# Taking a weight page's high and low rooms apart in a planned matmul kernel, with new planner constants

## The chip, the cores and the metric

The kernel runs on one core of a Trainium2 chip. The metric is the device time of one execution in microseconds; the time of a kernel is the median of its runs.

## What is computed

The reference is a two-layer encoder trunk over 256 tokens of width 4096, in float32:

```
for l in range(DEPTH):                       # 2 layers
    h = rmsnorm(x, norm_w[l])
    proj = h @ w_in[l]                       # 256x4096 @ 4096x11264
    aq, ak, av, ag, rq, rk, rv, rg = split(proj)
    a_out = silu(ag) * gqa_attention(rope(rmsnorm(aq)), rope(rmsnorm(ak)), av)   # 16 heads of 128
    r_out = silu(rg) * rmsnorm(bidirectional_retention(rope(rq), rope(rk), rv))  # 8 heads, values of 256
    x = x + concat(a_out, r_out) @ w_out[l]  # 256x4096 @ 4096x4096
return rmsnorm(x, final_norm)
```

Nearly all the arithmetic is in the two projections.

## The kernel before, in words

**Products.** A float32 number is split into a high part (a cast to fp32r) and a low part (the number less its high part), and a product of two numbers is three matmuls on TensorE: high by high, low by high (both at L1458, with the page's high part moving), and high by low (L1468). Each moves 512 columns. The work on one stretch of 1024 output columns is a *block*: 11 blocks for the input projection and 4 for the output projection of each layer, one after the other. A block goes through 16 *pairs* of 128-row strips of the weights. Five or six of the pairs use seven products (Strassen's scheme, with sums of weights), the others eight products with a shared third operand. The products of a block add up in seven PSUM banks, M1 to M7. At the end of the block VectorE and ScalarE drain the banks into two SBUF tiles `ca` and `cb` (`combine`, L1475), and the next block's first product in a bank waits for its drain.

**Pages.** The weights come as pages of 128x1024 numbers. SyncE loads a raw page (`wraw`, five buffers, L447). ScalarE casts it to `whi`, VectorE makes `wlo = wraw - whi`; a seven-product pair has sums in `wsum` between. There are `RING = 5` buffers each of `whi` and `wlo`. Some pages are *far* (`fhi`, `flo`, one buffer, L492): ScalarE makes both the high part and its negative, and a DMA on GpSimd's queue adds the raw weights onto it (L505). `parts` (L473) takes a room for both parts of a page, emits the cast, and puts the making of the low part on a list (`later`) that is worked off when the plan has time, at the latest when TensorE takes the page. `begin` (L510) starts a page; it is called in `end_product` (L1413) when the last product of an older page is finished, that is, after its last L1468 matmul, for the page that comes five later.

**Groups.** The loop at L1438 takes up to `TOGETHER = 4` products that read the same page: first the two L1458 matmuls of each, then the L1468 matmul of each.

**The order.** Every engine's queue is written out in Python, in program order, by a planner. It keeps a model clock (`Now`) that advances 0.2268 us for a matmul of 512 columns, and model clocks of VectorE and ScalarE (`Clock`, with `V_FIXED`, `S_FIXED` and a cost for each element). All other work (splitting the operands for the next phase, rotary embeddings, the attention's scores and values, retention, norms) is written as generators, *lanes*, that yield the time for which they want to rest. After each product `tick` (L892) steps the lanes that are due, as long as `room` (L558) finds that VectorE and ScalarE can take another step (`STEP_V`, `STEP_S`) and still make the coming pages in time, with a reserve of `1.25 + 2 * PASS + MARGIN`, less `RUSH` in the first output block of a layer. In the first `TIGHT_A` and last `TIGHT_B` products of a block a step is taken only if both engines are nearly idle. `need` (L747) and `take` (L544) force work that has come too late. A lane that has a matmul next rests `PE_REST` after its last vector work (L848); a PSUM bank for lanes is taken as free `2 * PASS` after its last reader (L823). A tile stored to HBM and fetched again is expected `FETCH` after the fetch is issued (L1149, L1105), other loads after `LANDING`; a far page `FAR_LANDING` after its cast; the far page's DMA is put into GpSimd's queue when its cast is at most `ADD_AHEAD` away (L555). The constants move no instruction by themselves: a wait in the program is always for the true producer, and the constants decide only in which order the instructions stand.

**Output tasks.** After an output block, `out_tasks` (L1558) issues two DMAs that add the residual, rests `LANDING`, and then runs `out_task` for each of the two 512-column halves.

**Last block.** In the last block, halves of the pages of five pairs are kept until the end in rooms of operands that are no longer needed; `dead_room` (L581) hands these out in an order written as a list of tags.

Of the kernel before, what the change touches and what calls it, by code (L numbers as in the profile page):

```python
# [12 lines left out]
F32R = mybir.dt.float32r  # L13
# [4 lines left out]
P = 128  # L18
# [9 lines left out]
NB = 512  # L28
# [4 lines left out]
NP = KT // 2  # L33
BLK = 32
ALL = slice(None)
# [3 lines left out]
RING = 5  # L39
FAR = 1  # L40

STEP_V = 1.6
STEP_S = 1.3

V_FIXED = 0.15
S_FIXED = 0.12

MM = {512: 0.2268, 256: 0.1177}
PASS = 0.2

LANDING = 11.0
STORE = 8.0
FETCH = 13.0
FAR_LANDING = 11.0
MARGIN = 0.0

RUSH = 1.5

EARLY = 0.7

ADD_AHEAD = 2.5

NEED = {"ak": 4, "ag": 3, "rk": 4, "rg": 4}

PE_REST = 1.5

TIGHT_A = 3
TIGHT_B = 5

AT_ONCE = 2  # L70

WARM = 20

SPLITS = 3

START = 1

# [2 lines left out]
MORE = (1,)  # L80

DELAYED = tuple([_p for _p in range(NP) if _p not in SEVEN + MORE][-5:])
# [129 lines left out]

EASY = ("M7",)

TOGETHER = 4
BANKS = ("M1", "M2", "M3", "M4", "M5", "M6", "M7", "M8")


class Now:


    t = 0.0
# [39 lines left out]
def hybrid_encoder(  # L262
# [15 lines left out]
    now = Now()  # L278
# [16 lines left out]
    def t(pool, shape, tag, bufs=None, dt=F32):  # L295
        kw = {} if bufs is None else {"bufs": bufs}
        return pool.tile(shape, dt, tag=tag, name=tag, **kw)
# [101 lines left out]
    class Weights:  # L399


        def __init__(self):
            self.pages = []
            for l in range(DEPTH):
                for w, n in ((w_in, N_IN), (w_out, N_OUT2)):
                    for b in range(n):
                        second = w is w_out
                        for g in GROUPS[second]:
                            start = (l, b) == (0, 0) and w is w_in
                            for slot in slots_of(g, second, start):  # L410
                                one = Page()
                                one.pair, one.kind, one.uses, one.left = slot[0][1], slot[0][3], len(slot), 3 * len(slot)
                                one.whole = start and one.pair in NATIVE
                                one.seven = one.pair in SEVENS[second] and not one.whole
                                one.far = is_far(g, one.pair, one.kind) and not (
                                    start and (g in GROUPS[0][:2] or one.whole)
                                )
                                one.src, one.begun, one.low_at, one.next = [], False, None, []
                                one.kept = None
                                if w is w_out and (l, b) == (DEPTH - 1, n - 1) and one.pair in DELAYED:  # L420
                                    one.kept = 0 if one.kind == PAGE_A else 1
                                    one.uses, one.left = one.uses - 1, one.left - 3
                                if one.kind == PAGE_A:
                                    one.src.append(w[l, b, one.pair, 0])
                                if one.kind == (PAGE_A if one.seven else PAGE_B):
                                    one.src.append(w[l, b, one.pair, 1])
                                self.pages.append(one)
            self.wholes = [g for g in self.pages if g.whole]
            near = [g for g in self.pages if not g.far and not g.whole]
            far = [g for g in self.pages if g.far]  # L430
            for g, then in zip(near, near[RING:]):
                g.next.append(then)
            for g, then in zip(near[RING : RING + FAR] + far, far):
                g.next.append(then)
            self.order = near[:RING]
            for g in self.pages:
                self.order += g.next
            self.todo = [src for g in self.order for src in g.src]
            self.loaded, self.at = 0, 0
            self.raw, self.later, self.adds = [], [], []  # L440
# [20 lines left out]
                self.later.pop(0)[1]()  # L461
            return self.raw.pop(0)

        def places(self, g, hi, lo, halves=(ALL,)):

            g.hi, g.lo = ({h: v[:, h, :] for h in (0, 1, ALL)} for v in (hi, lo))
            if g.kept is None:
                return halves
            for v in (g.hi, g.lo):
                v[g.kept] = dead_room()  # L470
            return (1 - g.kept, g.kept)

        def parts(self, g, src, halves=(ALL,), then=None):  # L473

            hi = t(wp, [P, 2, NB], "whi", RING, F32R)
            lo = t(wp, [P, 2, NB], "wlo", RING, F32R)
            halves = self.places(g, hi, lo, halves)
            for h in halves:
                ac.copy(g.hi[h], src[:, h, :])
            g.high_at = ac.until + PASS  # L480

            def low():
                ve.after(g.high_at)
                for h in halves:
                    ve.tensor_sub(g.lo[h], src[:, h, :], f32(g.hi[h]))
                g.low_at = ve.until + PASS
                if then:
                    then()

            self.later.append((g, low))  # L490

        def far_parts(self, g, src):  # L492

            hi = t(wp, [P, 2, NB], "fhi", FAR, F32R)
            lo = t(wp, [P, 2, NB], "flo", FAR, F32R)
            halves = self.places(g, hi, lo)
            for h in halves:
                ac.copy(g.hi[h], src[:, h, :])
            for h in halves:
                ac.activation(g.lo[h], f32(g.hi[h]), AF.Copy, scale=-1.0)  # L500
            g.high_at, g.low_at = ac.until, ac.until + FAR_LANDING

            def add():
                for h in halves:
                    nc.gpsimd.dma_start(g.lo[h], g.src[0][:, h, :], accum_op=ALU.add)  # L505

            self.adds.append((ac.until, add))
            self.load()
# [29 lines left out]
                self.later.pop(0)[1]()  # L538

        def low_parts(self, all=False):  # L540
            while self.later and (all or self.later[0][0].high_at <= max(now.t, ve.until) + 0.1):
                self.later.pop(0)[1]()

        def take(self):  # L544
# [34 lines left out]
    rooms = []  # L579

    def dead_room():  # L581

        if not rooms:
            e, o = len(EIGHTS), len(SEVENS[1])
            kinds = {
                "x3": ("x3", e, [P, 2, 2, P], "p k s t -> p (k s t)"),
                "x8h": ("x8h", e, [P, 2, SEQ], "p k s -> p (k s)"),
                "x8l": ("x8l", e, [P, 2, SEQ], "p k s -> p (k s)"),
                "x7h": ("x7h", o, [P, 7, P], "p k t -> p (k t)"),
                "x7l": ("x7l", o, [P, 7, P], "p k t -> p (k t)"),  # L590
            }
            order = "x7h x7l x3 x3 x7h x7l x7h x7l x3 x8h x8l x7h x7l x3 x8h x8l x7h x7l x3 x7h" if MORE else "x3 x3 x8h x8l x3 x3 x8h x8l x7l x7h x3 x3 x8h x8l x3 x3 x8h x8l x7l x7h"
            rooms.extend(kinds[v] for v in order.split())
        tag, bufs, shape, flat = rooms.pop(0)
        return t(ap, shape, tag, bufs, F32R).rearrange(flat)[:, :NB]

# [750 lines left out]
    def block(after_pair, phase, then, first_order=False, order=LAST_ORDER, last=None, plain=False, hurried=False):  # L1347
# [65 lines left out]
        def end_product(n, name, p, index, k, h):  # L1413
            g = pages[p, k]
            follow()
            if n == final[name]:
                finished.append((name, partial(last or combine, name, acc, c)))
                if name == order[0] or n == len(flat) - 1:
                    follow(True)
            if not at_last or name != order[-1] or p not in DELAYED:  # L1420
                g.uses -= 1
            if not g.uses and g in using:
                using.remove(g)
                if g.whole:
                    for _ in range(1 if g is not weights.wholes[-1] else RING):
                        begun()
                for one in g.next:
                    weights.begin(one)
            tick()
            left[p] -= 1  # L1430
            if not left[p]:
                done.append(p)
            while done and all(not left[q] for q in range(min(done))):
                q = min(done)
                done.remove(q)
                after_pair(q)

        n = 0  # L1438
        while n < len(flat):
# [5 lines left out]
            for one in group:  # L1445
# [9 lines left out]
                else:  # L1455
# [3 lines left out]
                    now.t += 2 * MM[NB]  # L1459
                    g.left -= 2  # L1460
                    low.append((one, a[0]))
                    if one is not group[-1]:
                        tick()
            for one, a in low:
# [93 lines left out]
    def out_tasks(l, n, c):  # L1558
        for i in range(2):
            nc.gpsimd.dma_start(c[i], residual(l, 2 * n + i), accum_op=ALU.add)  # L1560
        yield LANDING
        for i in range(2):
            yield from out_task(l, 2 * n + i, c[i])

    def last_combine(res):

# [240 lines left out]
```

## Time and profile before

| | |
|---|---|
| median of 3 runs | 2627.58 us (2625.68 to 2627.82) |
| the profiled execution | 2625.96 us |
| its span, first to last instruction | 2623.8 us |
| TensorE matmul busy | 2601.0 us (99%), 11725 matmuls |
| VectorE busy | 2166.6 us (83%) |
| ScalarE busy | 1804.2 us (69%) |
| GpSimd busy | 372.9 us (14%) |
| mean DMA rate | 261 GB/s, 683.94 MB |

The profile comes from one execution, whose own time is 2.2 us above its span. PE is TensorE's matmuls, DVE VectorE, ACT ScalarE, POOL GpSimd, SP SyncE. L247 is the planner's recording helper, through which all DVE and ACT work goes, so its instructions are told apart by their tiles.

### The profile page before, as it was taken

How to read it: one execution, taken by the hardware profiler on the slowest of the kernel's cores; microseconds unless marked ns; L12 is line 12 of the kernel's file. 1: busy time of each engine (PE TensorE's matmuls, PEld its weight loads, DVE VectorE, ACT ScalarE, POOL GpSimd, SP SyncE). 2: the span in 40 equal slices, each digit the busy share in tenths (PEclk: the TensorE clock that was granted, in tenths of full speed). 3: DMA queues.
4: the chain of work that ended last, by engine and by line, in shares of the span. 5: the costliest groups of instructions: out<-in, count | busy, mean ns of one | idle time of the engine just before them, and what ended most of it. 6: DMA issues, size and time to landing. Idle time of an engine off the chain costs nothing.

```text
span 2623.8 us, 34532 instructions
## 1 busy us (share of the span) xinstructions
PE 2601.0 (99%) x11725; PEld 2154.2 (82%) x11725; DVE 2166.6 (83%) x2684; ACT 1804.2 (69%) x2576; POOL 372.9 (14%) x510
## 2 busy tenths in 40 slices
PE   9999999999999999999999999999999999999998
PEld 7788888888888888888878888888888888888886
DVE  7898887798778898877978878888887688987876
ACT  8676676667565788655877666776576557876655
POOL 0012211221111101111111111211210111010000
PEclk9999999999999999999999999999999999999999
DMA  9988888887778777889988888888877787788887
GB/s 305 285 262 285 272 271 284 270 269 243 235 238 249 239 249 237 274 262 281 311 246 259 271 274 283 266 273 288 280 231 217 245 258 239 221 259 264 254 249 228
DMA packets 201121, 683.94 MB, mean 261 GB/s; under 512 B 24176, under 2 KB 30832, under 8 KB 200944
## 3 DMA queue, kind: packets, MB, share of 16 engines
q1 hardware_dynamic: 147760, 521.27, 56.3%
q0 software_dynamic: 53184, 160.46, 26.5%
q8 instruction: 92, 1.51, 0.2%
q14 instruction: 85, 0.70, 0.1%
HBM read 637.60 MB, written 44.04 MB: 260 GB/s over the span
## 4 chain that ended last, share of the span: by engine, by line
PE 92%; issue 1%; DMA 1%; ACT 1%; DVE 1%; POOL 0%; POOLq 0%; DVEq 0%; ACTq 0%
PE M L1458 59%; PE M L1468 30%; PE ps L973 1%; PE ps L974 1%; PE ps L975 1%; DMA q<-q_dram 1%; PE ps L1458 0%; DMA wraw<-in_w_in 0%; DVE wlo L247 0%; ACT ca L247 0%; DVE ca L247 0%; PE ps L1468 0%; DVE cb L247 0%; ACT pr L247 0%; ACT whi L247 0%
## 5 line engine op out<-in xcount | busy, mean ns | idle before, releaser
L247 ACT CAST whi<-wraw 128x1024 fp32r<-128x1024 f32 (+1 forms) x808 | 768.7, 962 | 463.0 <-PE M L1458 310.3
L247 DVE TENSOR_TENSOR wlo<-wraw,whi 128x1024 fp32r<-128x1024 f32 (+1 forms) x808 | 886.9, 1110 | 236.6 <-ACT whi L247 230.9
L1458 PE MATMUL M<-whi,x8h 128*128 128x512 f32 x1340 | 521.9, 389 | 0.0
L1458 PE MATMUL M<-whi,x8l 128*128 128x512 f32 x1340 | 521.5, 389 | 0.0
L1458 PE MATMUL M<-whi,x7h 128*128 128x512 f32 x1265 | 493.9, 390 | 3.7 <-DVE ca L247 2.5
L1458 PE MATMUL M<-whi,x7l 128*128 128x512 f32 x1265 | 492.9, 390 | 0.0
L247 ACT CAST whi<-wsum 128x1024 fp32r<-128x1024 f32 x314 | 329.6, 1050 | 137.1 <-PE M L1458 93.8
L1468 PE MATMUL M<-wlo,x8h 128*128 128x512 f32 x1340 | 420.2, 389 | 0.0
L247 DVE TENSOR_TENSOR wlo<-wsum,whi 128x1024 fp32r<-128x1024 f32 x314 | 382.5, 1218 | 38.7 <-ACT whi L247 36.8
L1468 PE MATMUL M<-wlo,x7h 128*128 128x512 f32 x1265 | 407.8, 389 | 1.1 <-DVE wlo L247 1.1
L1458 PEld LDWEIGHTS M<-whi,x8h 128*128 128x128 f32 x1340 | 251.6, 188 | 51.7 <-issue 0.2
L1458 PEld LDWEIGHTS M<-whi,x8l 128*128 128x128 f32 x1340 | 251.6, 188 | 51.7 <-issue 0.2
L1468 PEld LDWEIGHTS M<-wlo,x8h 128*128 128x128 f32 x1340 | 251.2, 188 | 51.7
L1458 PEld LDWEIGHTS M<-whi,x7h 128*128 128x128 f32 x1265 | 237.8, 188 | 55.7 <-DVE ca L247 2.9
L1468 PEld LDWEIGHTS M<-wlo,x7h 128*128 128x128 f32 x1265 | 237.5, 188 | 50.5 <-DVE wlo L247 1.5
L1458 PEld LDWEIGHTS M<-whi,x7l 128*128 128x128 f32 x1265 | 238.0, 188 | 48.9
L1458 PE MATMUL M<-whi,x 128*128 128x512 f32 x840 | 258.9, 389 | 0.7 <-ACT whi L247 0.7
L505 POOL DMA_DIRECT2D flo<-in_w_in x108 | 97.3, 901 | 1044.4 <-ACT flo L247 1001.4
L247 ACT CAST fhi<-wraw 128x1024 fp32r<-128x1024 f32 (+1 forms) x148 | 154.7, 1045 | 99.8 <-PE M L1458 93.9
L247 DVE TENSOR_TENSOR wsum<-wraw 128x1024 f32<-128x1024 f32 x157 | 191.2, 1218 | 18.7 <-DMA wraw<-in_w_out 11.3
L1458 PEld LDWEIGHTS M<-whi,x 128*128 128x128 f32 x840 | 157.1, 188 | 32.9 <-ACT whi L247 1.1
L1458 PE MATMUL M<-fhi,x8h 128*128 128x512 f32 x440 | 171.3, 389 | 0.0
(301 smaller groups left out, 3282.9 us busy)
## 6 DMA issues: line engine op xcount, KB each, us to landing
wraw<-in_w_in SPq DMA_DIRECT2D x700, 512.0 KB, 5.0
wraw<-in_w_out SPq DMA_DIRECT2D x256, 512.0 KB, 5.2
flo<-in_w_in POOLq DMA_DIRECT2D x108, 512.0 KB, 7.9
flo<-in_w_out POOLq DMA_DIRECT2D x38, 512.0 KB, 8.8
full<-next_dram POOLq DMA_DIRECT2D x18, 512.0 KB, 7.7
p_dram<-room POOLq DMA_DIRECT2D x64, 128.0 KB, 4.6
pT<-p_dram POOLq DMA_DIRECT2D x16, 512.0 KB, 8.1
next_dram<-room POOLq DMA_DIRECT2D x40, 128.0 KB, 5.9
```

What stands on the lines that cost most here:

```text
L247: return call(out, *args, **kwargs)
L505: nc.gpsimd.dma_start(g.lo[h], g.src[0][:, h, :], accum_op=ALU.add)
L973: nc.tensor.matmul(out, a[0], b[0], start=start, stop=False)
L974: nc.tensor.matmul(out, a[0], b[1], start=False, stop=False)
L975: nc.tensor.matmul(out, a[1], b[0], start=False, stop=stop)
L1458: nc.tensor.matmul(acc[name], a[i], g.hi[h], start=m == first[name] and not i, stop=False)
L1468: nc.tensor.matmul(acc[name], a, g.lo[h], start=False, stop=m == final[name])
```

## The change

A page's high room and low room are taken apart. `begin` may now be called for the next page as soon as the last high matmul of an older page is emitted (`SOON`), with `low_free` false; the low part's room is taken when the low part is made, which waits until the older page's last low matmul is emitted. Thirteen of the planner's constants get other values. The rooms of the last block's kept halves are handed out in the order in which the pairs end. `out_tasks` has a scheduling point between its two DMAs and between its two halves.

```diff
-STEP_S = 1.3
-V_FIXED = 0.15
-S_FIXED = 0.12
+STEP_S = 1.0
+V_FIXED = 0.12
+S_FIXED = 0.15
-PASS = 0.2
+PASS = 0.3
-FETCH = 13.0
-FAR_LANDING = 11.0
-MARGIN = 0.0
-RUSH = 1.5
+FETCH = 11.0
+FAR_LANDING = 13.0
+MARGIN = 0.6
+RUSH = 1.0
-ADD_AHEAD = 2.5
+ADD_AHEAD = 1.5
-PE_REST = 1.5
-TIGHT_A = 3
-TIGHT_B = 5
+PE_REST = 2.0
+TIGHT_A = 4
+TIGHT_B = 2
-SPLITS = 3
+SPLITS = 2
+APART = 0.0
+SOON = True
...
-        def places(self, g, hi, lo, halves=(ALL,)):
-            g.hi, g.lo = ({h: v[:, h, :] for h in (0, 1, ALL)} for v in (hi, lo))
+        def places(self, g, part, v, halves=(ALL,)):
+            v = {h: v[:, h, :] for h in (0, 1, ALL)}
+            setattr(g, part, v)
             if g.kept is None:
                 return halves
-            for v in (g.hi, g.lo):
-                v[g.kept] = dead_room()
+            v[g.kept] = dead_room()
             return (1 - g.kept, g.kept)
         def parts(self, g, src, halves=(ALL,), then=None):
-            hi = t(wp, [P, 2, NB], "whi", RING, F32R)
-            lo = t(wp, [P, 2, NB], "wlo", RING, F32R)
-            halves = self.places(g, hi, lo, halves)
+            halves = self.places(g, "hi", t(wp, [P, 2, NB], "whi", RING, F32R), halves)
             for h in halves:
                 ac.copy(g.hi[h], src[:, h, :])
             g.high_at = ac.until + PASS
             def low():
+                assert g.low_free
+                self.places(g, "lo", t(wp, [P, 2, NB], "wlo", RING, F32R))
                 ve.after(g.high_at)
...
         def low_parts(self, all=False):
-            while self.later and (all or self.later[0][0].high_at <= max(now.t, ve.until) + 0.1):
+            while self.later and self.later[0][0].low_free and (all or self.later[0][0].high_at <= max(now.t, ve.until) + 0.1):
...
                 for one in g.next:
-                    weights.begin(one)
+                    one.low_free = True
+                    if not one.begun:
+                        weights.begin(one)
...
                     low.append((one, a[0]))
+                    if one is group[-1] and g.uses == len(group) and SOON:
+                        for then in g.next:
+                            if not then.far and not then.begun:
+                                then.low_free = False
+                                weights.begin(then)
...
     def out_tasks(l, n, c):
         for i in range(2):
             nc.gpsimd.dma_start(c[i], residual(l, 2 * n + i), accum_op=ALU.add)
-        yield LANDING
-        for i in range(2):
-            yield from out_task(l, 2 * n + i, c[i])
+            if i < 1:
+                yield APART
+        second = now.t + LANDING
+        yield max(0.0, LANDING - APART)
+        yield from out_task(l, 2 * n, c[0])
+        yield max(0.0, second - now.t)
+        yield from out_task(l, 2 * n + 1, c[1])
```

## Rows read from the trace of the kernel before

**Rows 1.** Busy time by stretches: window, us; PE (x), PEld, DVE, ACT, POOL; PEclk, DMA, GB/s.

```profile
0.00:100.00 100.00, 95.97 (x389) 72.72 (x390) 81.35 (x122) 78.55 (x135) 3.84 (x8) 0.99 0.91 309
...
200.00:300.00 100.00, 100.00 (x459) 83.48 (x458) 84.31 (x102) 70.63 (x106) 20.56 (x29) 1.00 0.87 283
...
1300.00:1400.00 100.00, 96.55 (x422) 78.52 (x421) 80.46 (x109) 79.69 (x129) 9.06 (x11) 1.00 0.82 245
...
2600.00:2624.00 24.00, 12.38 (x55) 9.93 (x53) 13.04 (x26) 6.79 (x14) 1.13 (x2) 0.86 0.47 176
sum 2624.00, PE 2601.00 PEld 2154.21 DVE 2166.59 ACT 1804.18 POOL 372.92; mean PE 96.33 PEld 79.79 DVE 80.24 ACT 66.82 POOL 13.81
```

**Rows 2.** What PE waited for: us in total, times, longest us.

```profile
PE M L1468 <- DVE wlo L247: 2.8, 2, 1.7
PE M L1458 <- DVE ca L247: 2.5, 3, 1.0
PE ps L973 <- ACT pr L247: 2.0, 2, 1.0
PE M L1458 <- DVE cb L247: 1.2, 1, 1.2
...
PE M L1458 <- ACT whi L247: 0.7, 1, 0.7
```

**Rows 3.** Timeline of PE at the first block's end (start, us, what); last, granted clock.

```profile
94.40 0.39 PE L1458 MATMUL M<-whi,x7l 128*128 128x512 f32 x1
95.85 0.50 PE L1468 MATMUL M<-wlo,x7h 128*128 128x512 f32 x1 [1.06 <-DVE wlo L247]
97.58 0.50 PE L1458 MATMUL M<-whi,x7h 128*128 128x512 f32 x1 [1.23 <-DVE cb L247]
...
98.30:101.70 3.40, 3.40 (x10) 2.64 (x9) 3.40 (x5) 2.58 (x6) 0.00 (x0) 0.50 1.04 269
```

**Rows 4.** Timeline of ACT and DVE ahead of these waits.

```profile
88.39 1.05 ACT L247 CAST whi<-wraw 128x1024 fp32r<-128x1024 f32 x1 [4.52 <-DMA wraw<-in_w_in]
...
89.47 1.23 DVE L247 TENSOR_TENSOR wlo<-wraw,whi 128x1024 fp32r<-128x1024 f32 x1 [1.85 <-ACT whi L247]
...
94.58 1.22 DVE L247 TENSOR_TENSOR wlo<-wsum,whi 128x1024 fp32r<-128x1024 f32 x1
```

**Rows 5.** Timeline of DVE and PE at a later block's end.

```profile
1316.38 1.22 DVE L247 TENSOR_TENSOR wlo<-wraw,whi 128x1024 fp32r<-128x1024 f32 x1
1317.51 0.68 DVE L247 TENSOR_TENSOR ca<-ca,M 128x512 f32<-128x512 f32 x1
...
1318.25 0.50 PE L1458 MATMUL M<-whi,x7h 128*128 128x512 f32 x1 [1.00 <-DVE ca L247]
```

**Rows 6.** Timeline of ACT and PE at an attention head's scores.

```profile
345.76 0.56 ACT L247 ACTIVATE pr<-ps,st,rs 128x256 f32<-128x256 f32 x1 [2.33 <-DVE st L247]
...
347.01 0.38 PE L973 MATMUL ps<-kv,aqh 128*128 128x256 f32 x1 [1.00 <-ACT pr L247]
```

**Rows 7.** Timeline of ACT and PE early in the second layer.

```profile
1351.61 1.05 ACT L247 CAST fhi<-wraw 128x1024 fp32r<-128x1024 f32 x1
...
1355.97 0.73 PE L1458 MATMUL M<-whi,x 128*128 128x512 f32 x2 [0.71 <-ACT whi L247]
...
1359.83 0.50 PE L1468 MATMUL M<-wlo,x 128*128 128x512 f32 x1 [1.75 <-DVE wlo L247]
```

**Rows 8.** The fetched queries: ACT, PE, DMA's times to landing, ACT's waits.

```profile
517.87 1.14 ACT L247 CAST aqh<-q 128x512 fp32r<-128x512 f32 x2 [4.25 <-DMA q<-q_dram]
...
518.54 0.39 PE L973 MATMUL ps<-kv,aqh 128*128 128x256 f32 x1 [0.19 <-ACT aqh L247]
...
DMA to landing us min/median/max: 5.7/11.3/14.0
...
ACT aqh L247 <- DMA q<-q_dram: 10.2, 4, 4.3
```

**Rows 9.** Waits for a page's old rooms, and GpSimd's waits for far pages.

```profile
POOL flo L505 <- ACT flo L247: 1462.9, 128, 37.6
ACT whi L247 <- PE M L1458: 404.0, 421, 4.7
...
ACT whi L247 <- PE M L1468: 28.7, 13, 4.2
```

More of the change, by code (lines that the diff above doesn't have):

```diff
@@ L417, in __init__ @@
                                 )
-                                one.src, one.begun, one.low_at, one.next = [], False, None, []
+                                one.src, one.begun, one.low_at, one.next, one.low_free = [], False, None, [], True
                                 one.kept = None
@@ L495, in far_parts @@
             lo = t(wp, [P, 2, NB], "flo", FAR, F32R)
-            halves = self.places(g, hi, lo)
+            self.places(g, "hi", hi)
+            halves = self.places(g, "lo", lo)
             for h in halves:
@@ L591, in dead_room @@
             }
-            order = "x7h x7l x3 x3 x7h x7l x7h x7l x3 x8h x8l x7h x7l x3 x8h x8l x7h x7l x3 x7h" if MORE else "x3 x3 x8h x8l x3 x3 x8h x8l x7l x7h x3 x3 x8h x8l x3 x3 x8h x8l x7l x7h"
-            rooms.extend(kinds[v] for v in order.split())
+            for p in range(NP):
+                if p not in EIGHTS:
+                    rooms.extend(kinds[v] for v in ("x7h", "x7l"))
+                else:
+                    rooms.extend(kinds[v] for v in ("x3", "x8h", "x8l")[: 3 if p in EIGHTS[2:] and p not in DELAYED else 1])
         tag, bufs, shape, flat = rooms.pop(0)
```

## The prediction

> **What bounds the kernel now.** I read the busy time by stretches of 100 us first. TensorE is the bound: of the 27 stretches 20 read as the second row here, 100.00 of 100.00, and its idle time is 2623.8 - 2601.0 = 22.8 us in all [rows 1]. Of that 11.6 us lie after the last matmul (12.38 busy in the last 24) and 4.0 in the first 100 us. The change takes no matmul away, so the 11725 matmuls stay as they are, at 0.227 us from start to start where PE runs on. What can be won is what stands between them.
>
> The second view is the list of what PE waited for. It is short: 2.8 us for low parts, 2.5 and 1.2 us for banks being drained, 2.0 us for the softmax's reading of a lane's bank, 0.7 us for a high part [rows 2]. A row's idle time is counted from the modelled end of the matmul before, 0.389 us after its start, so a wait costs 0.389 - 0.227 = 0.16 us more than it shows. The third view is the timeline around each wait. Four kinds come out:
>
> **A, the end of the first block.** From 94.40 to 95.85 and on to 97.58 the matmuls are 1.45 and 1.73 us apart in place of 0.23: 2.7 us lost [rows 3]. The granted clock then reads 0.50, the lower of the two levels, for 3.4 us, which costs half of that, 1.7 us. Together 4.4 us. DVE is behind there: it waited 1.85 us for a cast that waited 4.52 us for a raw page to land, and so made the wanted low part at 94.58, five us later, behind bank drains and weight sums [rows 4].
>
> **B, other block ends.** Three waits for `ca`, 2.5 us [rows 2], with 3 x 0.16 on top 3.0 us. At 1316 DVE made a low part for 1.22 us first and drained the bank after it, and PE waited 1.00 us [rows 5].
>
> **C, scores.** Two waits of 1.0 us, 2.3 us with the 0.16 each: PE stood before the second head's scores until ACT had read the bank of the first [rows 6].
>
> **D, early in the second layer.** 0.71 us for a high part and 1.75 us for a low part, 2.8 us with the 0.16 each [rows 7]. ACT had far pages, squares and copies in its queue ahead of the page.
>
> A to D come to 4.4 + 3.0 + 2.3 + 2.8 = 12.5 us. With 0.7 us lost on a late query (below) it is 13.2 us, 0.5% of the time, and that is the most that any reordering can bring.
>
> **The change, part by part.** *Beginning the high part earlier.* By its words it frees the high room before the group's low matmuls, up to 4 x 0.227 = 0.9 us earlier. The chip does most of that already: ACT waited 421 times for an L1458 matmul to free `whi`, and 13 times for an L1468 one [rows 9]. The wait was always for the old high part's own reader. What the change moves is the cast's place in ACT's queue, ahead of what `tick` steps during the low matmuls, and the planner's belief of when the page is ready, so that the low part follows directly when its room comes free. Where ACT is ahead of PE this gives nothing. Where a page is late it gives between 0 and 0.9 us for each; I take 0.9 for each of D's two waits, cut by the wait itself to 0.7 + 0.9 = 1.6 us. The upper end is all of D, 2.8.
>
> What is queued behind: an early cast that waits for PE holds ACT's later work. The 421 waits are 404.0 us, 0.96 us each [rows 9]. If a score's exponential stands behind such a cast, the next head's scores are late by about that. C shows two such delays; I price a new order at 0.7 us for new delays of this sort, between 0 and four of 1.0 us. The Trainium skill, "TensorE: Matmul & The Clock Gate", section "Architectural detail", says that ACT and DVE are strict first-in-first-out, which speaks against any early start that has to wait. The trace agrees as far as these waits show it. By that rule alone this part would be a loss of up to 4 us, not a gain.
>
> *Reserve in `room`.* It grows by 2 x 0.1 (`PASS`) + 0.6 (`MARGIN`) = 0.8 us for DVE; for ACT 0.3 less of `STEP_S` leaves 0.5 us. In the hurried block it grows by another 0.5 (`RUSH`). `TIGHT_A` 3 to 4 keeps one more product at a block's start free of side work. Against it stands `TIGHT_B` 5 to 2: three products at the end, some 2 us, in which side work may now be put ahead of the drains. For B I take two thirds, 2.0 us of 3.0 (between 0 and 3.0): the reserve of 0.8 us nearly covers waits of 1.0, and the looser end takes some of it back. For A I take half, 2.2 us of 4.4 (0 to 4.4): its root is a raw page that landed late, and raw pages are neither loaded sooner nor given another buffer, but the drains and the low part behind them can be ordered otherwise.
>
> *Scores.* `PE_REST` + 0.5 and the bank's 2 x 0.1 put the product up to 0.7 us later behind other matmuls. For each of C's two waits that is 0.7 of 1.0: 1.4 us (0 to 2.3). Lanes get slower, but they are used many microseconds later.
>
> *Fetches.* `FETCH` 13 to 11 goes the wrong way for the queries: they land 5.7 to 14.0 us after issue, median 11.3 [rows 8]. Already at 13, ACT stood four times, 10.2 us, and the 4.25 us at 517 cost PE 0.7 us (two waits of some 0.2, with the 0.16 each). With the cast placed 2 us earlier that one hold becomes 6.3 us and costs PE 0.7 + 2 = 2.7; the others stay under 4.25 us, which PE's lead in pages bears. So +2.0 us. Ends: 0, if the queries are fetched into a quieter stretch, and 8, if four casts each cost 2 us.
>
> *Far pages.* `FAR_LANDING` + 2 and `ADD_AHEAD` - 1 I cost at nothing: PE has no wait for `flo` [rows 2]. GpSimd stood 1462.9 us before these DMAs, 128 times [rows 9]; issuing them up to 1 us later in the plan shortens the hold for stores and fetches queued behind. If the cover of the far pages' early start went, PE would wait for `flo` by name.
>
> *The rest.* `SPLITS` 3 to 2 lets two operand splits run side by side in place of three; the scheduling points in `out_tasks` put its second DMA on GpSimd's queue a step later; `V_FIXED` and `S_FIXED` change the model by 0.03 us for an instruction. Each only reorders; they are in the 0.7 us. The kept rooms hold what was held before, and the 11.6 us after the last matmul are a chain that no part of the change touches.
>
> **The sum.** - 2.2 (A) - 2.0 (B) - 1.4 (C) - 1.6 (D) + 2.0 (queries) + 0.7 (new delays) = - 4.5 us. Against the profiled execution's own 2625.96 that is 2621.5. The median of the runs is 1.6 us higher, so 2627.58 - 4.5 = 2623.1.
>
> **The rivals.** *Nearly all stalls go.* If the earlier pages and larger reserve also end A, and queries land in time, 8 to 13 us come back: about 2617. For it: all waits are of 1 to 2 us, the size of the reserve added. Against: A hangs on a landing, and it alone holds a third of the sum. *The stalls only move.* Each constant reorders hundreds of instructions, and the list names some ten waits that the old plan did not foresee [rows 2]; a new plan may have its own. About 2627, within 2 us of before. For it: the early start is largely done by the chip already [rows 9]. *Slower: the fetches bind.* If most of the 8 query fetches are met by a cast that was put in ACT's queue too early, holds pass 4.25 us, the point at which PE began to lose [rows 8], and each costs up to 2 us: with half the gains gone that is about + 8 us, 2635. For it: the median landing of 11.3 is above the new 11. Against: landing varies, and four of the eight did not hold ACT even at 13. That the change does nothing can be left out, since the order of all queues changes.
>
> **How the numbers follow.** Forecast 0.50, nearly all 0.18, only moved 0.20, slower 0.12. A measurement of this kernel can tell about 0.2%, 5.3 us, from no change, so faster means under 2622.3. The forecast of 2623.1 lies near that line: with 2.5 us either way it gives 0.20 to faster and 0.30 to same. Faster 0.20 + 0.18 = 0.38, same 0.30 + 0.20 = 0.50, slower 0.12. The range goes from 2616.0, nearly all of the 12.5 us back, to 2630.0, half the fetches' price with no gain.
>
> **What would show it.** Right: PE's idle time near 18 us; the waits for `ca` and for `pr` under 1 us in sum; the early waits of the second layer shortened; the waits for `whi` still on L1458; the hold of ACT for `q` longer than 10.2 us in sum. If clock 0.50 no longer appears after the first block, A is gone and the first rival gains. Wrong: PE waits for `flo`, for `aqh` or for operands (`x8h`, `x7h`) of more than 2 us each, or a list of new waits as long as the old one.

## The result, and the profile after

The changed kernel takes 2631.22 us (median of 12 runs, 2629.77 to 2639.65), the kernel before 2625.96 us (12 runs beside them). The ratio is 1.0025, with an interval of 1.0018 to 1.0033: slower by about 6 us, where 4.5 us less was forecast. The profiled execution of the changed kernel took 2632.53 us, its span is 2630.8 us, 7.0 us more than before.

Busy time by stretches of the changed kernel, columns as in [rows 1]:

```profile
0.00:100.00 100.00, 98.74 (x407) 75.69 (x408) 84.42 (x126) 81.20 (x135) 3.82 (x8) 1.00 0.91 316
...
900.00:1000.00 100.00, 96.58 (x427) 78.98 (x426) 89.27 (x135) 78.32 (x123) 11.99 (x15) 0.98 0.78 243
...
1300.00:1400.00 100.00, 98.10 (x430) 79.97 (x429) 83.12 (x113) 82.66 (x136) 8.82 (x11) 1.00 0.83 249
...
2200.00:2300.00 100.00, 96.62 (x433) 79.37 (x432) 90.10 (x135) 76.57 (x123) 12.02 (x15) 0.98 0.76 237
...
sum 2631.00, PE 2605.12 PEld 2155.49 DVE 2172.11 ACT 1809.59 POOL 369.90; mean PE 96.49 PEld 79.83 DVE 80.45 ACT 67.02 POOL 13.70
```

The first 100 us and the stretch from 1300 are better than in [rows 1] (98.74 after 95.97, 98.10 after 96.55). Two stretches are new among the bad ones, 900 to 1000 and 2200 to 2300, and each also has a mean clock of 0.98. What PE waited for, beside [rows 2]:

```profile
PE M L1468 <- DVE ca L251: 6.8, 4, 2.6
PE M L1483 <- DMA flo<-in_w_out: 1.6, 3, 1.0
PE M L1468 <- DVE cb L251: 1.5, 4, 0.9
...
PE M L1483 <- DMA x7h<-in_w_out: 1.0, 1, 1.0
PE ps L981 <- DVE D L251: 0.9, 2, 0.5
PE ps L983 <- DVE aql L251: 0.8, 4, 0.2
```

(L1468 and L1483 are what L1458 and L1468 were.) The waits for low parts, for `pr` and for `whi` are gone. The wait for `ca` has grown from 2.5 to 6.8 us, its longest from 1.0 to 2.6. Both long ones are at the *hand-over* from the input blocks to the output blocks of a layer. VectorE and PE at the first:

```profile
975.52 0.68 DVE L251 TENSOR_TENSOR ca<-ca,M 128x512 f32<-128x512 f32 x1
976.12 1.22 DVE L251 TENSOR_TENSOR wlo<-wsum,whi 128x1024 fp32r<-128x1024 f32 x1
977.26 1.22 DVE L251 TENSOR_TENSOR wsum<-wraw 128x1024 f32<-128x1024 f32 x1
978.39 0.68 DVE L251 TENSOR_TENSOR ca<-ca,M 128x512 f32<-128x512 f32 x1
...
976.23 0.40 PE L1483 MATMUL M<-wlo,x7h 128*128 128x512 f32 x1
979.22 0.77 PE L1468 MATMUL M<-whi,x7h 128*128 128x512 f32 x1 [2.60 <-DVE ca L251]
```

and the busy time of the 3.4 us after it, columns as in [rows 1]:

```profile
978.90:982.30 3.40, 3.08 (x7) 2.48 (x8) 3.37 (x5) 2.26 (x4) 0.00 (x0) 0.51 0.00 0
```

VectorE has no idle time. Between the two drains into `ca` stand a low part and a weight sum `wsum`, 1.14 us from start to start each. The sum belongs to a page that comes five pages later, and PE stands for the second drain from 976.23 to 979.22, 3.0 us in place of 0.23. The granted clock then reads 0.51, the lower level, for 3.4 us, as it did after the first block before [rows 3]. In the kernel before, the sum stands behind the last drain, and PE does not wait at the same place:

```profile
980.24 0.68 DVE L247 TENSOR_TENSOR ca<-ca,M 128x512 f32<-128x512 f32 x1
980.84 1.22 DVE L247 TENSOR_TENSOR wsum<-wraw 128x1024 f32<-128x1024 f32 x1
...
981.07 0.47 PE L1458 MATMUL M<-whi,x7h 128*128 128x512 f32 x1
```

There `begin` runs in `end_product` after the drain was emitted; in the changed kernel it runs before the low matmuls of the group, and so before the drain. The page that is begun at the end of every block before an output block is the first page of a seven-product pair, whose `begin` starts with this sum.

Counted from start to start, the two hand-overs lose 2.76 + 2.75 us in these gaps, 1.3 us in four smaller ones and 2 x 1.7 us at half clock, 10.2 us in all; the kernel before had 1.0 there (at 2278), so that is some 9 us more. Gone are A with its half clock (4.4 us), C (2.3) and D (2.8), 9.5 us. The 7.0 us of the span are about what is left over: other block ends (+1.6 us), far and kept pages (+3.3), late queries (+1.0) and scores of the retention (+1.3).

### The profile page after: what moved, and what is told of

The parts are those of the page before. It is cut to its first block, busy times and chain, and to the rows that moved or that the text cites. A ratio compares the mean times of both kernels' runs of the same rounds, so it can differ in the third digit from the quotient of the medians.

```text
span 2630.8 us, 34613 instructions
## 1 busy us (share of the span) xinstructions
PE 2605.1 (99%) x11725; PEld 2155.5 (82%) x11725; DVE 2172.1 (83%) x2684; ACT 1809.6 (69%) x2576; POOL 369.9 (14%) x510
## 4 chain that ended last, share of the span: by engine, by line
PE 82%; DMA 5%; DVE 2%; issue 2%; ACT 1%; POOL 0%; POOLq 0%; DVEq 0%; ACTq 0%
PE M L1468 53%; PE M L1483 26%; DMA q<-q_dram 2%; DMA flo<-in_w_out 2%; PE ps L983 1%; PE ps L981 1%; PE ps L982 1%; DVE wlo L251 1%; DMA q_dram<-cb 0%; DMA full<-next_dram 0%; DVE cb L251 0%; DMA wraw<-in_w_out 0%; DMA x7h<-in_w_out 0%; DVE wsum L251 0%; DVE ca L251 0%
## 5 line engine op out<-in xcount | busy, mean ns | idle before, releaser
L1468 PE MATMUL M<-whi,x8h 128*128 128x512 f32 x1340 | 522.1, 390 | 0.0
L1468 PE MATMUL M<-whi,x8l 128*128 128x512 f32 x1340 | 521.7, 389 | 0.0
L1468 PE MATMUL M<-whi,x7h 128*128 128x512 f32 x1265 | 495.0, 391 | 8.5 <-DVE ca L251 6.8
L1468 PE MATMUL M<-whi,x7l 128*128 128x512 f32 x1265 | 493.5, 390 | 0.0
L1483 PE MATMUL M<-wlo,x8h 128*128 128x512 f32 x1340 | 419.0, 389 | 0.0
L1483 PE MATMUL M<-wlo,x7h 128*128 128x512 f32 x1265 | 408.1, 390 | 0.0
L1468 PEld LDWEIGHTS M<-whi,x8h 128*128 128x128 f32 x1340 | 251.7, 188 | 51.1 <-issue 0.2
L1468 PEld LDWEIGHTS M<-whi,x8l 128*128 128x128 f32 x1340 | 251.7, 188 | 51.1 <-issue 0.2
L1483 PEld LDWEIGHTS M<-wlo,x8h 128*128 128x128 f32 x1340 | 251.0, 188 | 51.8
L1468 PEld LDWEIGHTS M<-whi,x7h 128*128 128x128 f32 x1265 | 238.2, 188 | 61.9 <-issue 6.0
L1483 PEld LDWEIGHTS M<-wlo,x7h 128*128 128x128 f32 x1265 | 238.1, 188 | 49.5 <-DVE wlo L251 0.5
L1468 PEld LDWEIGHTS M<-whi,x7l 128*128 128x128 f32 x1265 | 238.4, 188 | 48.6
L1468 PE MATMUL M<-whi,x 128*128 128x512 f32 x840 | 258.9, 389 | 0.0
L1468 PEld LDWEIGHTS M<-whi,x 128*128 128x128 f32 x840 | 157.7, 188 | 32.9 <-ACT whi L251 0.4
L1468 PE MATMUL M<-fhi,x8l 128*128 128x512 f32 x440 | 171.3, 389 | 0.0
```

Of the source, the lines that this page charges most:

```text
L1468: nc.tensor.matmul(acc[name], a[i], g.hi[h], start=m == first[name] and not i, stop=False)
L1483: nc.tensor.matmul(acc[name], a, g.lo[h], start=False, stop=m == final[name])
```

## The experiments

Three theories went into the first four runs. **M**: the early begin puts the weight sum ahead of the last drain, and that is what the change loses. **C**: the new constants let work pile up on VectorE before the hand-over. **F**: the far pages' late landing. Each ratio is against the kernel before.

**Early begin off, new constants kept.**

```diff
-SOON = True
+SOON = False
```

> The changed kernel with the early begin switched off and all thirteen new constants kept. Theory M (the early begin puts a weight sum of 1.1 us ahead of the block's last drain on VectorE, and the half clock follows): the waits for ca near 976 and 2280 us fall from 2.6 us to about 1.5 or less, the clock stays at 1.00 there, and the time falls by 4 to 8 us, to a ratio of about 1.000 against the kernel before. Theory C (the new constants let side work pile up on VectorE before the hand-over, and the sum's place is secondary): the waits at 976 and 2280 stay above 2 us, the ratio stays at 1.002 or more. Theory F (the far pages' late landing is what costs): the waits for flo tell whether the early begin or the constants made them; 3.2 us are at stake.

Measured: 2653.87 us, ratio 1.0101 (1.0083 to 1.0119): 23 us slower than the changed kernel. That is far above what any of the theories gave. The waits at the hand-overs did fall, to 1.44 and 1.45 us, but half clock came at both all the same. PE's waits, the first hand-over and the stretch after it:

```profile
PE ps L981 <- DVE wsum L251: 7.1, 5, 1.5
PE M L1468 <- DVE ca L251: 7.0, 6, 1.7
PE ps L981 <- ACT pr L251: 3.6, 5, 1.0
PE M L1483 <- DVE wlo L251: 2.9, 3, 1.8
...
PE M L1483 <- DMA flo<-in_w_out: 1.9, 2, 1.3
```

```profile
989.77 0.68 DVE L251 TENSOR_TENSOR ca<-ca,M 128x512 f32<-128x512 f32 x1
990.37 1.23 DVE L251 TENSOR_TENSOR wsum<-wraw 128x1024 f32<-128x1024 f32 x1
...
990.60 0.56 PE L1468 MATMUL M<-whi,x7h 128*128 128x512 f32 x1 [1.44 <-DVE ca L251]
...
990.80:994.20 3.40, 3.40 (x9) 2.67 (x9) 3.40 (x4) 2.49 (x4) 0.00 (x0) 0.51 0.01 5
```

Counted from start to start, the two hand-overs lose 9.3 us, though the sum stands behind the drain and no page is begun early. So VectorE also comes late to the drains for a reason that is not the sum's place, as theory C has it. The rest of the plan is another one: the scores (`ps`, L981) wait for VectorE and ScalarE, ten times. This run therefore cannot price the early begin. It has waits for `flo` without it, which speaks against the early begin as their cause.

**New code, constants as before.** All thirteen lines of constants back:

```diff
-STEP_S = 1.0
+STEP_S = 1.3
...
-SPLITS = 2
+SPLITS = 3
```

> The changed kernel's code with the early begin, with all thirteen constants as before. Theory M: both hand-overs from input to output blocks show a wait for ca of 2 us or more and a stretch at half clock, some 5 us each, whatever the constants are; ratio about 1.002. Theory C: no wait for ca over 1.2 us at the hand-overs, ratio 1.000 or less. Theory F: waits for flo of over 1 us in sum if the early begin makes them, none if FAR_LANDING or ADD_AHEAD do.

Measured: 2661.58 us, ratio 1.0126 (1.0105 to 1.0147). The hand-overs lose 4.3 and 4.7 us with half clock, as M expects and C does not. Of the longest wait for `ca`, 2.6 us, the sum accounts for 1.14; the rest comes here under the old constants, so the new constants alone are not what makes VectorE late. And half of the 35 us above the kernel before is something else:

```profile
PE M L1468 <- ACT x L251: 16.7, 2, 8.4
PE M L1468 <- DVE ca L251: 6.5, 5, 2.6
PE M L1483 <- DVE wlo L251: 3.1, 3, 1.7
...
PE M L1483 <- DMA flo<-in_w_in: 1.8, 3, 0.8
```

Twice PE stands 8.4 us for a third operand `x` of the last pairs in the first output block: the plan makes operands too late. `flo` is waited for here too, with the old `FAR_LANDING` and `ADD_AHEAD`.

**Early begin everywhere but at a block's end.** This pair isolates the sum's place: no queue differs from the changed kernel's but VectorE's, and there only by the order of sum and last drain at eight block ends.

```diff
-                    if one is group[-1] and g.uses == len(group) and SOON:
+                    if one is group[-1] and g.uses == len(group) and SOON and n + len(group) < len(flat):
```

> The changed kernel, but without the early begin after the last group of a block; the only difference in any queue is that at eight block ends the last drain stands ahead of the weight sum on VectorE. Theory M: at 976 and 2280 the wait for ca falls by the sum's 1.14 us, from 2.6 to about 1.5, the clock stays at 1.00, and each hand-over loses 2 us in place of 5: 5 to 7 us less in all, ratio about 1.000. Theory C: the waits fall by the 1.14 us alone and the half clock stays: 2.3 us less, ratio 1.0016. Theory F: the waits for flo stay as they are, 1.6 us, in either case.

Measured: 2626.67 us (12 runs), ratio 0.9998 (0.9987 to 1.0008), 4.6 us less than the changed kernel and the same as the kernel before. At the first hand-over:

```profile
975.84 1.22 DVE L251 TENSOR_TENSOR wlo<-wsum,whi 128x1024 fp32r<-128x1024 f32 x1
976.98 0.69 DVE L251 TENSOR_TENSOR ca<-ca,M 128x512 f32<-128x512 f32 x1
977.58 1.22 DVE L251 TENSOR_TENSOR wsum<-wraw 128x1024 f32<-128x1024 f32 x1
...
977.81 0.47 PE L1468 MATMUL M<-whi,x7h 128*128 128x512 f32 x1 [1.46 <-DVE ca L251]
```

and the stretch after the second hand-over, by busy time:

```profile
2277.80:2281.20 3.40, 3.40 (x9) 2.65 (x9) 3.37 (x4) 2.50 (x4) 0.00 (x0) 0.50 0.00 0
```

The wait falls from 2.60 to 1.46, by the sum's 1.14 us, in both places. After the first the clock stays up, as M has it; after the second it reads 0.50 in this execution, as C has it. The two hand-overs lose 6.8 us in place of 10.2. The 4.6 us of time lie between M's 5 to 7 and C's 2.3 and do not choose between them. What the pair shows is the sum's place itself: no other instruction changes its place, the intervals of the two ratios do not overlap, and with the sum behind the drain the change's loss against the kernel before is gone. It does not make the hand-overs what they were: 6.8 us are still lost there, against 1.0 in the kernel before. The waits for `flo`, which theory F left at 1.6 us, are 0.2 us in this trace.

**Early begin at block ends alone**, the same pair in the other direction, against the run with the early begin off:

```diff
-                    if one is group[-1] and g.uses == len(group) and SOON:
+                    if one is group[-1] and g.uses == len(group) and SOON and n + len(group) >= len(flat):
```

> The early begin after the last group of a block alone; against the run with the early begin off, the only difference is the weight sum ahead of the last drain at eight block ends. Theory M: the two hand-overs wait 1.1 us longer for ca, and the half clock comes with it: 4 to 7 us slower than that run. Theory C: 2.3 us slower, and no half clock, or half clock in both.

Measured: 2657.88 us, ratio 1.0116 (1.0098 to 1.0134), 4.0 us above that run: at M's lower end, though the four runs of each (2652.52 to 2657.11 there, 2656.27 to 2660.53 here) cannot tell that from C's 2.3. `ca` is waited for 9.4 us in place of 7.0, and half clock lasts 6.8 us at both hand-overs where it was 3.4. PE's waits, and the busy time of the first such stretch:

```profile
PE M L1468 <- DVE ca L251: 9.4, 6, 2.6
```

```profile
987.70:994.50 6.80, 5.85 (x14) 4.68 (x15) 6.77 (x9) 5.60 (x9) 0.00 (x0) 0.50 0.40 142
```

So in a second plan the same eight swaps cost some 4 us. Not all of it need be theirs: half clock also doubled from 3.4 to 6.8 us at 1332, where no drain was swapped.

**Which bank is waited for.** A next set took the hand-over further. An output block uses M2 with its fifth product and M4 with its seventh, but the block ahead of it finishes M4 first. The swap:

```diff
+        elif order is LAST_ORDER and then % 2 == 0:
+            order = ("M3", "M5", "M2", "M4")
```

Put on the run without the early begin at block ends:

> The run without the early begin at block ends, and before an output block M2 is finished and drained ahead of M4 instead of after it. Theory M (what PE waits for at a hand-over is M2, the last bank drained and the fifth product of the next output block; M4 is the seventh): the waits for ca at 976 and 2280 fall below 0.5 us, no half clock, 3 to 5 us less than that run: about 2623, ratio 0.9985. Rival B (VectorE is behind on all drains there, so PE waits for another bank as long): within 1 us of that run, ratio 1.000.

Measured: 2624.96 us, ratio 0.9999 (0.9990 to 1.0008). At 979 PE now waits 0.21 us for the drain, and no half clock comes at either hand-over (timeline, then busy time):

```profile
977.52 1.22 DVE L251 TENSOR_TENSOR wlo<-wsum,whi 128x1024 fp32r<-128x1024 f32 x1
978.66 0.68 DVE L251 TENSOR_TENSOR ca<-ca,M 128x512 f32<-128x512 f32 x1
...
979.40 0.50 PE L1470 MATMUL M<-whi,x7h 128*128 128x512 f32 x1 [0.21 <-DVE ca L251]
```

```profile
974.00:982.00 8.00, 7.24 (x28) 4.61 (x27) 8.00 (x11) 3.96 (x5) 0.00 (x0) 1.00 0.50 126
```

The place is right, the size was too high: 1.7 us less than without the swap, which the runs can't tell from nothing. The two hand-overs lose 3.6 us in place of 6.8, but the trace of this run also has 1.4 us for a low part at 1253 that the other had not. It is 6 us under the changed kernel and level with the kernel before.

The swap on the changed kernel alone:

> The changed kernel with nothing but M2 finished and drained ahead of M4 before an output block; the weight sum still stands ahead of the last drain, which is now M4's. Theory M: the sum costs nothing where it stands, since M4 is wanted two products (0.9 us or more) later; the hand-overs lose under 1.5 us each in place of 5, about 7 us less than the changed kernel: 2624, ratio 0.999. Rival B: PE waits for M4 instead, 2 us or more with the half clock, ratio 1.002 or more.

Measured: 2626.32 us, ratio 1.0000 (0.9991 to 1.0009), 4.9 us less than the changed kernel. The sum still stands ahead of the last drain, but this is M4's now:

```profile
979.22 1.21 DVE L251 TENSOR_TENSOR wsum<-wraw 128x1024 f32<-128x1024 f32 x1
980.36 0.68 DVE L251 TENSOR_TENSOR ca<-ca,M 128x512 f32<-128x512 f32 x1
...
981.09 0.50 PE L1470 MATMUL M<-whi,x7h 128*128 128x512 f32 x1 [1.34 <-DVE ca L251]
```

PE waits 1.34 us in place of 2.60, and the clock stays at 1.00. It did not cost nothing, as M said, but about half.

The swap on the kernel before:

> The kernel before with M2 finished and drained ahead of M4 before an output block. Theory M: the 1.0 us at 2278 goes, nothing else moves: 0.5 to 2 us less, ratio 0.9995. Rival B: no change at 2278, ratio 1.000.

Measured: 2627.28 us, ratio 1.0002 (0.9992 to 1.0012). The wait at 2278 is gone from the trace, 1.0 us of 2627, and the time cannot show it.

**Is a plan's time the constants' doing?** The first two runs were 23 and 30 us off the changed kernel, so the next ones moved one constant to its neighbour.

```diff
-V_FIXED = 0.12
+V_FIXED = 0.13
```

> The changed kernel with V_FIXED at 0.13 in place of 0.12: the model charges VectorE 10 ns more for an instruction, which is below anything that the engines could feel. Theory L (a plan's time is largely luck of which stalls its order meets, and the constants chosen are one lucky draw): 5 us or more away from the changed kernel, with stalls in other places, though the hand-overs still show the long wait for ca. Theory P (the constants describe the engines, and nearby values give nearby times): within 3 us, ratio 1.0015 to 1.0035.

Measured: 2666.44 us, ratio 1.0153 (1.0137 to 1.0169), 35 us more, for 10 ns in the model. PE waits for third operands in three places:

```profile
PE M L1468 <- DVE x L251: 12.4, 3, 4.4
PE M L1468 <- ACT x L251: 7.7, 3, 2.7
PE M L1468 <- DVE ca L251: 7.6, 5, 2.6
```

The neighbours of the kernel before, `V_FIXED` at 0.14 and 0.16 in place of 0.15:

> The kernel before with V_FIXED at 0.14 in place of 0.15, 10 ns of the model's charge for an instruction of VectorE. Theory L (the chosen constants are a lucky draw, and a neighbour is an ordinary one): 10 us or more above the kernel before. Theory P (nearby values give nearby times): within 4 us of it.

> The kernel before with V_FIXED at 0.16, the neighbour on the other side. Theory L: 10 us or more above the kernel before, with stalls that the other neighbour doesn't have. Theory P: within 4 us.

Measured: 2627.22 us at 0.14, ratio 1.0002 (0.9990 to 1.0013), and 2657.61 us at 0.16, ratio 1.0111 (1.0074 to 1.0147). One neighbour is as good as the kernel before, though much of its order is another, the other 31 us worse, with waits for `x` again (15.8 us on ScalarE's). The changed kernel's other neighbour, 0.11:

> The changed kernel with V_FIXED at 0.11, on the other side from the run at 0.13 that took 35 us more. Theory L: 5 to 40 us above the changed kernel, in other places than that run. Theory P with a limit between 0.12 and 0.13: within 4 us of the changed kernel.

Measured: 2649.19 us, ratio 1.0067 (1.0043 to 1.0091), 18 us above the changed kernel, with hand-overs of 5.8 and 8.3 us and a wait of 2.3 us for `flo`. Of four neighbours three lie 18 to 35 us higher and one level: theory L holds for most, not for each.

**The queries' rest.** One step of the forecast on its own:

```diff
-FETCH = 11.0
+FETCH = 13.0
```

> The changed kernel with FETCH back at 13 and nothing else. The forecast's step (a cast for a late query placed 2 us later holds ScalarE 2 us less): ScalarE's waits for q fall from 20.0 us to about 10, PE's waits for aql go, 1 to 2 us less if the rest of the plan stood still. Theory L: the rest doesn't stand still, and the time lands 5 us or more above the changed kernel.

Measured: 2632.67 us, ratio 1.0027 (1.0014 to 1.0041), the same as the changed kernel. ScalarE's waits for the queries, 20.0 us in seven with `FETCH` at 11, do not occur, and PE's 0.8 us for `aql` neither. The rows of the changed kernel, the last with the times to landing:

```profile
ACT aqh L251: 20.0, 7
...
PE ps L983: 0.8, 4
...
DMA to landing us min/median/max: 5.9/12.4/14.0
```

The 1 us came back and other waits took its place (1.1 us for a high part at 1371, 0.7 us for `flo` at 1710). The hand-overs have their waits of 2.60 and 2.59 us as in the changed kernel, but in this execution the clock stays up after the second:

```profile
2284.90:2288.30 3.40, 3.39 (x15) 2.81 (x16) 3.37 (x5) 1.96 (x4) 0.00 (x0) 1.00 0.12 18
```

**Constants that move nothing.** With all else as in the changed kernel, putting `TIGHT_B` or `STEP_S` alone back leaves every queue of the program as it is, and `ADD_AHEAD` moves a few DMAs on GpSimd's queue alone.

## Why the prediction was wrong

The bound was read rightly: TensorE is busy 99% before and after, nothing of its work changed, and all that moved were waits of up to 3 us and stretches at half clock.

**A** (2.2 of 4.4 us back): under-sized. The first block's end has no wait and no half clock any more, so all of it came back; PE ran through from 93.8 to 100 without a gap. That belongs to this draw of constants: with the new code and the old constants the waits and the half clock are there again, at 94 and 98.5.

**C** (1.4 of 2.3) and **D** (1.6 of 2.8): right in direction, under-sized; both are gone. Together with A some 9 us were gained where 5.2 were forecast.

**B** (2.0 of 3.0 back): this is the step that failed. In its place came a loss of 9 us at the hand-overs and 1.6 us at other block ends. Two things were wrong in it.

The first is what the early begin puts ahead of what. The forecast costed it as a cast on ScalarE and asked what is queued behind that cast. But `begin` issues more than a cast: for the first page of a seven-product pair it issues a sum on VectorE. VectorE is the engine that drains the banks, and it had no idle time at a block's end [rows 4, 5]. The run with the sum moved behind the last drain (4.6 us less) shows this, since no other instruction changes its place; the run with the sum moved ahead in another plan (4.0 us more) and the one with another bank drained last (4.9 us less) agree. The rule of the Trainium skill that the prediction cited ("TensorE: Matmul & The Clock Gate", "Architectural detail": ACT and DVE run their queues strictly in order) was the right rule, weighed on the wrong one of its two engines: the drain behind the sum came 1.14 us later. On ScalarE the early begin cost nothing that shows: 472 casts waited 447.3 us for PE, 0.95 us each, against 421 of 0.96 [rows 9], while the waits for `pr` went.

The second is the larger reserve in `room`, which was to cover waits of 1.0 us. It covered none. Of the three waits for `ca` before, those of 0.59 us at 186 and 1.00 us at 1318 stand as they were, and the third, at 2278, grew:

```profile
181.64 0.50 PE L1468 MATMUL M<-whi,x7h 128*128 128x512 f32 x1 [0.59 <-DVE ca L251]
...
1320.14 0.50 PE L1468 MATMUL M<-whi,x7h 128*128 128x512 f32 x1 [1.01 <-DVE ca L251]
```

The sum's place makes up 3.4 of the 9 us at the hand-overs. The rest, VectorE's coming late to the drains, is there with the early begin off and the new constants (9.3 us), and a wait of 2.6 us is there with the early begin on and the old constants; what makes it was not settled. That the change ends level with the kernel before once the sum is moved is because what A, C and D gave back pays for that rest.

**TIGHT_B** was taken as what speaks against B. Put back alone, it moves no instruction.

**Queries** (+2.0): right mechanism, over-sized. ScalarE's waits doubled from 10.2 us in four [rows 8] to 20.0 us in seven; from start to start PE lost 1.7 us on them in place of 0.7, so 1.0 us more.

**Far pages** (nothing): wrong by 3 us in the profiled execution, 1.6 us of idle for `flo` and 1.0 for a kept half. Runs with either half of the change undone have waits for `flo` too, and the run without the early begin at block ends, with the same GpSimd queue, has 0.2 us of them and 1.1 us for the kept half. Three plans with the old code have 0.9 to 1.4 us for `flo` as well, one of them the kernel before with nothing but the bank swap. What makes them was not settled.

**New delays** (+0.7, up to 4): the retention's scores cost 1.3 us, a wait for VectorE. The price was read off C as a score's exponential standing behind an early cast, and C does not show that: before it ScalarE stood idle 2.33 us for VectorE's `st` [rows 6].

The rival on the slower side named fetches that bind; the loss came by another way, the one the text listed as a wait for drains and took for a gain. The rival of stalls that only move was nearest: some 9 us gone, some 16 us new. And the range rested on the thought that the terms of one plan carry over to the next. The two kernels and their four neighbours, 10 ns apart in one constant, span 40 us, from 2626 to 2666, so the honest spread of "constants chosen anew", without a sight of the new order, reached some 40 us on the slow side, where the range allowed 2.4 us above the median of before (half of the fetches' 8 us, by which it was set, would have been 4).

What stays open: whether beginning high parts early is worth anything by itself. The change with its end of block mended is level with the kernel before, under other constants; the same constants without it are 27 us slower, but that is within what a plan's luck gives.

## What to carry to other kernels

When a step is called earlier, list every instruction that it issues on every engine, and ask of each which work that someone waits for it now stands ahead of; a page's "begin" was a cast in the description and a VectorE sum in the code. At a change of phase, finish and drain the buffers in the order in which the next phase takes them. Where a planner writes the queues from a model, treat a set of constants as one draw: judge a code change by runs that leave all other queues as they are, and expect the neighbour of a chosen draw to be worse (three of four were here).

## What the runs showed that was not expected

A change of 10 ns in the model's charge for an instruction moved the time by 35 us (1.0153), and three of the four slowest plans have one face: PE waits, up to 8.4 us at once, for third operands. And the same gap is not always followed by the lower clock level. After a gap of 2.6 us at a hand-over the changed kernel shows 3.4 us of it in both places, the run with `FETCH` at 13 in one of two; after 1.46 us the run without the early begin at block ends shows it in one of two. So the gap's length alone does not decide it, and what a hand-over costs differs by some 1.7 us with it.
